# A fourth seven-product chunk pair in each feed-forward block, its raw-weight split put first, and the read-back cast queued behind a weight cast

## Chip, cores and metric

One core of one Trainium2 chip. The metric is the device time of one execution, in microseconds (us); lower is better. Three runs of the kernel before gave 2432.48, 2436.15 and 2436.17 us.

## What is computed

The forward pass of two layers of a transformer-like trunk on 256 tokens of width 2048, in float32. Each layer does `x += mixer(rmsnorm(x))`, `x += swiglu(rmsnorm(x))` and a gated embedding term; a last RMSNorm ends it. The change is in the feed-forward part alone:

```python
def _swiglu(h, norm_g, w_gate, w_up, w_down):
    xn = _rmsnorm(h, norm_g)
    return (jax.nn.silu(xn @ w_gate) * (xn @ w_up)) @ w_down
```

The hidden width is 5632, so `w_gate` and `w_up` are 2048 x 5632 and `w_down` is 5632 x 2048, in each of the two layers. The batch is one sequence, two tiles of 128 tokens.

## The kernel before

**Matmuls.** Float32 products are made of three matmuls in a reduced format. A weight tile is split into a high part (`whi`, a cast on ScalarE, ACT, L106) and a low part (`wlo`, the raw tile minus the high part, on VectorE, DVE, L107), and the activations are held split in the same way. The product is high x high, high x low and low x high: three matmuls of 128x128 by 128x512 into one PSUM bank. Splits are made for two chunks of 128 rows at a time (1024 columns). `whi` and `wlo` have four buffers each.

**Units.** `unit` (L209) loads four chunks (1 MB) by one DMA on SyncE's queue (SP, L218) into a raw tile, splits them in two halves, and runs 24 matmuls: four chunks, two token tiles, three matmuls. There are three raw tiles in turn; a transfer into one waits for the splits that read it last. After each half `tick` counts one, and may run one piece of deferred work from a queue (`later`), which names the least number of ticks to wait. Program order is a priority for the tile scheduler, which then fixes an order on each engine's queue by its own model of time; each engine works through its queue in order.

**Feed-forward.** `ffn` (L827) goes over 11 blocks of 512 hidden columns in groups of three (the last group has two). For each block it makes gate and up (`gate_up`), and from the second group on the down products of the group before are done in between: one or two "down blocks" of 12 chunks (72 matmuls, three units) after each block. So blocks 0 to 3 follow each other without one, block 3 is followed by one, and so on; four stand behind the last block.

**Block 0** is all units (`gate_up_8`). During its second half `sums_of_operand` (L835) makes four combinations of the first `2 * NS` chunks of the activations, and splits them into `ST`.

**Blocks 1 to 10** (`gate_up_7`, L880) take the first `2 * NS` chunks in pairs. A pair is two chunks times two weights (gate, up) times two token tiles: eight products, which are made from seven by a scheme of the kind of Strassen's. `pair` (L851) loads the raw weights of two chunks of gate and of up by two DMAs (L855) into one raw tile, makes four sums of them on DVE in `T` (L858 with 1024 columns, L859 and L860 with 512 each), and splits seven pieces of 512 columns, two at a time, for seven products into seven PSUM banks (L849). The banks are B1 to B7. B1, B2 and B4 use the activations as they are, and B3, B5, B6 and B7 their combinations `ST`. The other chunks are done by units, `classical`, in the banks of B2, B4, B3 and B22; a unit stands between any two pairs.

With `NS = 3` a block has three pairs (63 matmuls) and units over chunks 6 to 15 of each weight: four units of four chunks and two of two (120 matmuls), 183 in all. Two units stand between the pairs and the rest behind them. Behind the last pair the shared sums are formed from B1, B5, B6 and B7 in `E` (a copy on ACT at L893, DVE at L894 to L897). L902 adds banks 0 and 1 (gate), then, when the units of the up weight are done, banks 2 and 3. L906 is the silu and L931 the product with the gate. `T` and `E` share one buffer, `work`.

**Turning the hidden block.** `cross` (L138) transposes the block of hidden values in 32x32 tiles on DVE (L143), writes it to DRAM by four DMAs of GpSimd's queue (POOL, L147) and reads it back by two (L151) as `tx`. `split_hid` (L919) splits what came back into `hH` (a cast on ACT, L921) and `hL` (DVE, L922), the stationary operand of the down blocks. `cross` is deferred by two ticks behind the block, and `split_hid` until 16 ticks behind `cross`:

```python
            later(lambda: x.update(x=cross(sl, fp)), key=("xT", i, b))
            later(lambda: split_hid(hT[gi], x["x"], 4 * n), key=("hT", i, b), after=(("xT", i, b), 16))
```

A pair makes two ticks, a unit of four chunks two, a unit of two chunks one. A block makes 16, a down block six.

Of the kernel before, what the change touches and what calls it, by code (L numbers as in the profile page):

```python
# [27 lines left out]
def trunk_kernel(ctx: ExitStack, tc: tile.TileContext, x, p, even_norm, even_w_in, even_w_gk,  # L28
# [74 lines left out]
    got_gains = turn_gains(0, graw)  # L103

    def split_sb(raw, hi, lo):
        nc.scalar.copy(hi, raw)  # L106
        nc.vector.tensor_tensor(lo, raw, hi.bitcast(F32), OP.subtract)  # L107


# [711 lines left out]

    NS = 3
    B2, B4, B3, B22, B1, B5, B6, B7 = range(8)

    def ffn(i, xs, nkey, nx_fn, fp):  # L827
# [19 lines left out]
        def product(p, stat, hi, lo, first, last):  # L847
            for m, (a, b) in enumerate(((stat[0], hi), (stat[0], lo), (stat[1], hi))):
                nc.tensor.matmul(bank[:, p], a, b, start=first and m == 0, stop=last and m == 2)  # L849

        def pair(j, b):  # L851

            raw = raw_tile().rearrange("p (r c) n -> p r c n", r=2)
            for c, w in enumerate((ffn_w_gate[i], ffn_w_up[i])):
                nc.sync.dma_start(raw[:, :, c], w[2 * j * P:(2 * j + 2) * P, b * NB:(b + 1) * NB]  # L855
                                  .rearrange("(k q) n -> q k n", q=P))

            nc.vector.tensor_tensor(T[:, 0:2], raw[:, 0], raw[:, :, 1], OP.add)  # L858
            nc.vector.tensor_tensor(T[:, 2], T[:, 1], raw[:, 0, 0], OP.add)  # L859
            nc.vector.tensor_tensor(T[:, 3], T[:, 2], raw[:, 1, 0], OP.add)  # L860

            def tok(c, t):
                return [x[:, 2 * j + c, t * P:(t + 1) * P] for x in xs]

            def comb(n):
                return [ST[:, hl, n, j] for hl in range(2)]

            pieces = [(raw[:, 0, 0:1], [(B1, tok(0, 0))]), (T[:, 0:2], [(B5, comb(0)), (B7, comb(2))]),
                      (T[:, 2:4], [(B6, comb(1)), (B4, tok(1, 1))]),
                      (raw[:, 1], [(B2, tok(1, 0)), (B3, comb(3))])]  # L870
            for n, (src, ps) in enumerate(pieces):
                hi = wp.tile([P, 2, NB], F32R, name="whi")
                lo = wp.tile([P, 2, NB], F32R, name="wlo")
                split_sb(src, hi[:, :len(ps)], lo[:, :len(ps)])
                for c, (p, stat) in enumerate(ps):
                    product(p, stat, hi[:, c], lo[:, c], j == 0, j == NS - 1 and p >= B1)
                if n % 2:
                    tick()

        def gate_up_7(b):  # L880
            need(("sT", i))
            rest = [(n, k) for n in range(2) for k in range(2 * NS, KC, KU)]

            def classical(n, k):
                nk = min(KU, KC - k)
                unit([bank[:, 2 * n], bank[:, 2 * n + 1]], xs, k, [((ffn_w_gate[i], ffn_w_up[i])[n], b * NB, NB)],
                     n == 1 and k == 2 * NS, k + nk == KC, nk=nk, begun=1)

            for j in range(NS):
                pair(j, b)  # L890
                if j < NS - 1:
                    classical(*rest.pop(0))
            nc.scalar.copy(E[:, 0], bank[:, B1])  # L893
# [24 lines left out]

        def split_hid(dst, x, k0):  # L919
            d = [dst[n][:, k0:k0 + 4, :].rearrange("p m (q r) -> p m q r", q=8) for n in range(2)]  # L920
            nc.scalar.copy(d[0], x)  # L921
            nc.vector.tensor_tensor(d[1], x, d[0].bitcast(F32), OP.subtract)  # L922

        def gate_up(gi, n):
# [7 lines left out]
                                               op1=OP.mult)  # L932
            x = {}
            later(lambda: x.update(x=cross(sl, fp)), key=("xT", i, b))
            later(lambda: split_hid(hT[gi], x["x"], 4 * n), key=("hT", i, b), after=(("xT", i, b), 16))

        def down(gi, cb, nx):
            for b in groups[gi]:
# [176 lines left out]
```

## Time and profile before

| | |
|---|---|
| median of three runs | 2436.15 us |
| lowest, highest | 2432.48, 2436.17 us |
| the profiled execution | 2435.57 us |
| its span in the trace | 2433.9 us |
| mean granted TensorE clock | 0.995 |
| TensorE (PE) busy | 2393.8 us |
| VectorE (DVE) busy | 1716.8 us |
| ScalarE (ACT) busy | 1258.4 us |
| GpSimd (POOL) busy | 105.6 us |

The profile is of one execution. PE is matmuls, and PEld the weight loads that overlap them. Matmuls overlap each other, so that a busy time is counted once and a matmul's own duration (0.39 us) is longer than the step from one to the next. The granted clock is what the throttle let TensorE have, as a share of full speed. "Idle before" an instruction is the time in which its engine did nothing ahead of it, with what ended that; a DMA lands later than the row of its issue. In the views below L849 is the matmuls of the pairs, and L235 to L237 those of the units.

### The profile page before, as it was taken

To read this page: it belongs to the slowest core of one execution; us is meant where nothing else is said; L and a number is where in the kernel's file an instruction comes from. 1 tells how busy PE (TensorE), PEld (TensorE's weight loads), DVE (VectorE), ACT (ScalarE), POOL (GpSimd) and SP (SyncE) were. 2 spreads that over 40 slices of the span, in tenths; PEclk is the share of its full clock that TensorE was granted. 3 is DMA by queue.
4 is the path that set the end of the run, shared out by engine and by line. 5 is a ranking of instruction groups with operands and counts; after the bars stand their busy time and mean duration, and the time that the engine had idled before them with its cause. 6 is when DMAs were issued, how large, how long until landed. Compare 5 with 4: busy or idle time off the path is not lost.

```text
span 2433.9 us, 28109 instructions
## 1 busy us (share of the span) xinstructions
PE 2393.8 (98%) x10786; PEld 1965.1 (81%) x10786; DVE 1716.8 (71%) x2009; ACT 1258.4 (52%) x1560; POOL 105.6 (4%) x177
## 2 busy tenths in 40 slices
PE   8999999999999999999999999999999999999998
PEld 7887788778887788888888888887788887888887
DVE  5765556888877877756666666568888788777565
ACT  6644445555545545446546565545554454454463
POOL 0000100100000000000000000000000000000000
PEclk9999999999999999999999999999999999999999
DMA  6454465566666666555554555555666666666563
GB/s 211 146 170 147 147 208 189 194 213 207 213 228 207 208 225 225 196 194 182 176 188 158 169 174 172 193 189 186 203 215 218 217 207 209 223 225 206 183 232 123
DMA packets 240681, 473.13 MB, mean 194 GB/s; under 512 B 12849, under 2 KB 19729, under 8 KB 240418
## 3 DMA queue, kind: packets, MB, share of 16 engines
q1 hardware_dynamic: 232514, 447.07, 55.5%
q0 software_dynamic: 7744, 23.08, 3.0%
q8 instruction: 84, 1.38, 0.2%
q10 hardware_dynamic: 288, 1.18, 0.1%
q14 instruction: 51, 0.42, 0.1%
HBM read 457.66 MB, written 13.63 MB: 194 GB/s over the span
## 4 chain that ended last, share of the span: by engine, by line
PE 71%; DVE 11%; DMA 10%; ACT 3%; issue 3%; SPq 0%; POOL 0%; DVEq 0%; POOLq 0%; ACTq 0%
PE bank L236 20%; PE bank L235 20%; PE bank L237 20%; PE bank L849 6%; DMA raw<-in_ffn_w_up_dram 6%; DVE wlo L107 6%; DMA raw<-in_odd_w_in_dram 2%; ACT whi L106 1%; DVE kT L135 1%; PE bank L165 1%; DVE work L858 1%; DMA raw<-in_ffn_w_down_dram 1%; DMA tx<-ty 1%; DVE sl L931 1%; DVE work L902 1%
## 5 line engine op out<-in xcount | busy, mean ns | idle before, releaser
L107 DVE TENSOR_TENSOR wlo<-raw,whi 128x1024 fp32r<-128x1024 f32 (+2 forms) x848 | 981.7, 1172 | 460.1 <-ACT whi L106 456.4
L106 ACT CAST whi<-raw 128x1024 fp32r<-128x1024 f32 (+2 forms) x848 | 842.3, 1011 | 830.6 <-PE bank L237 542.3
L235 PE MATMUL bank<-whi,aH 128*128 128x512 f32 (+2 forms) x2176 | 849.7, 391 | 0.7 <-ACT whi L106 0.7
L236 PE MATMUL bank<-wlo,aH 128*128 128x512 f32 (+2 forms) x2176 | 843.6, 388 | 5.0 <-DVE wlo L107 5.0
L237 PE MATMUL bank<-whi,aL 128*128 128x512 f32 (+2 forms) x2176 | 842.9, 388 | 0.0
L236 PEld LDWEIGHTS bank<-wlo,aH 128*128 128x128 f32 x2176 | 410.0, 188 | 89.5 <-DVE wlo L107 8.9
L235 PEld LDWEIGHTS bank<-whi,aH 128*128 128x128 f32 x2176 | 409.8, 188 | 84.9 <-issue 2.8
L237 PEld LDWEIGHTS bank<-whi,aL 128*128 128x128 f32 x2176 | 409.4, 188 | 84.9 <-issue 1.0
L235 PE MATMUL bank<-whi,hH 128*128 128x512 f32 x704 | 277.2, 394 | 0.0
L236 PE MATMUL bank<-wlo,hH 128*128 128x512 f32 x704 | 277.0, 393 | 0.0
L237 PE MATMUL bank<-whi,hL 128*128 128x512 f32 x704 | 273.6, 389 | 0.0
L106 ACT CAST whi<-work 128x1024 fp32r<-128x1024 f32 x120 | 126.3, 1053 | 199.5 <-PE bank L237 122.8
L107 DVE TENSOR_TENSOR wlo<-work,whi 128x1024 fp32r<-128x1024 f32 x120 | 146.7, 1222 | 58.0 <-ACT whi L106 57.6
L849 PE MATMUL bank<-whi,sT 128*128 128x512 f32 x480 | 170.2, 394 | 5.5 <-ACT whi L106 5.5
L235 PEld LDWEIGHTS bank<-whi,hH 128*128 128x128 f32 x704 | 132.2, 188 | 30.0
L237 PEld LDWEIGHTS bank<-whi,hL 128*128 128x128 f32 x704 | 132.1, 188 | 29.7
L236 PEld LDWEIGHTS bank<-wlo,hH 128*128 128x128 f32 x704 | 132.4, 188 | 26.1
L849 PEld LDWEIGHTS bank<-whi,sT 128*128 128x128 f32 x480 | 91.2, 190 | 25.3 <-ACT whi L106 6.3
L858 DVE TENSOR_TENSOR work<-raw 128x1024 f32<-128x1024 f32 x60 | 73.4, 1224 | 52.0 <-DMA raw<-in_ffn_w_up_dram 51.6
L147 POOL DMA_DIRECT2D ty<-tq x88 | 48.6, 559 | 1123.3 <-DVE tq L143 973.0
L849 PE MATMUL bank<-wlo,sT 128*128 128x512 f32 x240 | 94.8, 395 | 1.9 <-DVE wlo L107 1.9
L849 PE MATMUL bank<-wlo,aH 128*128 128x512 f32 x180 | 73.3, 407 | 10.8 <-DVE wlo L107 10.4
(253 smaller groups left out, 1623.9 us busy)
## 6 DMA issues: line engine op xcount, KB each, us to landing
raw<-in_ffn_w_down_dram SPq DMA_DIRECT2D x88, 1024.0 KB, 5.4
raw<-in_ffn_w_gate_dram SPq DMA_DIRECT2D x48, 1024.0 KB, 5.2
raw<-in_ffn_w_up_dram SPq DMA_DIRECT2D x48, 1024.0 KB, 5.2
raw<-in_odd_w_in_dram SPq DMA_DIRECT2D x48, 1024.0 KB, 5.1
raw<-in_ffn_w_gate_dram SPq DMA_DIRECT2D x80, 512.0 KB, 4.1
raw<-in_ffn_w_up_dram SPq DMA_DIRECT2D x80, 512.0 KB, 5.3
raw<-in_even_w_in_dram SPq DMA_DIRECT2D x36, 1024.0 KB, 5.1
raw<-in_ple_w_gate_dram SPq DMA_DIRECT2D x28, 1024.0 KB, 5.1
```

The source lines that it names most:

```text
L106: nc.scalar.copy(hi, raw)
L107: nc.vector.tensor_tensor(lo, raw, hi.bitcast(F32), OP.subtract)
L135: nc.vector.transpose(dst[32 * a:32 * a + 32, :, :, 32 * q:32 * q + 32], src.rearrange("p t (m a c) -> p t m a c", a=4, c=32)[32 * q:32 * ...
L147: nc.gpsimd.dma_start(y[:, :, q].rearrange("a c t n -> c a (t n)"), tq[32 * q:32 * q + 32].rearrange("c a t m r -> c a (t m r)"))
L165: nc.tensor.transpose(ps[:, c, tt, :], h[:, tt, k * P:(k + 1) * P], ident)
L235: nc.tensor.matmul(ps[tt][:, :n], sh, hi[:, c, :n], start=st, stop=False)
L236: nc.tensor.matmul(ps[tt][:, :n], sh, lo[:, c, :n], start=False, stop=False)
L237: nc.tensor.matmul(ps[tt][:, :n], sl, hi[:, c, :n], start=False, stop=en)
L849: nc.tensor.matmul(bank[:, p], a, b, start=first and m == 0, stop=last and m == 2)
L858: nc.vector.tensor_tensor(T[:, 0:2], raw[:, 0], raw[:, :, 1], OP.add)
L902: nc.vector.tensor_tensor(e, bank[:, 2 * n:2 * n + 2], e, OP.add)
L931: nc.vector.scalar_tensor_tensor(sl[:, tt], pu[tt], rs[:, tt:tt + 1], sl[:, tt], op0=OP.mult, op1=OP.mult)
```

## The change

`NS` goes from 3 to 4, so that a block takes chunks 0 to 7 in four pairs (84 matmuls) and chunks 8 to 15 in four units of four chunks (96 matmuls): 180 in all. Three of the units stand between the pairs, the third of them already a unit of the up weight, and one stands behind the last pair. Where a bank's accumulation ends is now worked out from what is left, since the gate's units end before the last pair. The combinations of the activations are four thirds as wide.

Within a pair the seven pieces are taken in another order. The first is now both gate weights as loaded (B1 and B2); then the first two sums are made and split (B5, B7), then the last two (B6, B4), and the last piece is one weight as loaded (B3). Before, all sums stood ahead of the first split, which was one weight (B1), and the last piece had two (B2, B3).

The cast of the hidden block read back, L921, gets an edge in ACT's queue behind the last weight cast that was traced before it (`state["cast"]`, kept by `split_sb`), and is traced 10 ticks behind `cross` in place of 16.

```diff
     def split_sb(raw, hi, lo):
-        nc.scalar.copy(hi, raw)
+        state["cast"] = nc.scalar.copy(hi, raw).ins
         nc.vector.tensor_tensor(lo, raw, hi.bitcast(F32), OP.subtract)
...
-    NS = 3
+    NS = 4
...
-        def pair(j, b):
+        def pair(j, b, rest):
...
-            nc.vector.tensor_tensor(T[:, 0:2], raw[:, 0], raw[:, :, 1], OP.add)
-            nc.vector.tensor_tensor(T[:, 2], T[:, 1], raw[:, 0, 0], OP.add)
-            nc.vector.tensor_tensor(T[:, 3], T[:, 2], raw[:, 1, 0], OP.add)
+            def sums_13():
+                nc.vector.tensor_tensor(T[:, 0:2], raw[:, 0], raw[:, :, 1], OP.add)
+
+            def sums_24():
+                nc.vector.tensor_tensor(T[:, 2], T[:, 1], raw[:, 0, 0], OP.add)
+                nc.vector.tensor_tensor(T[:, 3], T[:, 2], raw[:, 1, 0], OP.add)
...
-            pieces = [(raw[:, 0, 0:1], [(B1, tok(0, 0))]), (T[:, 0:2], [(B5, comb(0)), (B7, comb(2))]),
-                      (T[:, 2:4], [(B6, comb(1)), (B4, tok(1, 1))]),
-                      (raw[:, 1], [(B2, tok(1, 0)), (B3, comb(3))])]
-            for n, (src, ps) in enumerate(pieces):
+            pieces = [(None, raw[:, :, 0], [(B1, tok(0, 0)), (B2, tok(1, 0))]),
+                      (sums_13, T[:, 0:2], [(B5, comb(0)), (B7, comb(2))]),
+                      (sums_24, T[:, 2:4], [(B6, comb(1)), (B4, tok(1, 1))]),
+                      (None, raw[:, 1, 1:2], [(B3, comb(3))])]
+            for n, (made, src, ps) in enumerate(pieces):
+                if made:
+                    made()
...
                 for c, (p, stat) in enumerate(ps):
-                    product(p, stat, hi[:, c], lo[:, c], j == 0, j == NS - 1 and p >= B1)
+                    product(p, stat, hi[:, c], lo[:, c], j == 0,
+                            j == NS - 1 and (p >= B1 or not any(n == p // 2 for n, _ in rest)))
...
         def split_hid(dst, x, k0):
             d = [dst[n][:, k0:k0 + 4, :].rearrange("p m (q r) -> p m q r", q=8) for n in range(2)]
-            nc.scalar.copy(d[0], x)
+            with tc.issue_after(state["cast"]):
+                nc.scalar.copy(d[0], x)
             nc.vector.tensor_tensor(d[1], x, d[0].bitcast(F32), OP.subtract)
...
-            later(lambda: split_hid(hT[gi], x["x"], 4 * n), key=("hT", i, b), after=(("xT", i, b), 16))
+            later(lambda: split_hid(hT[gi], x["x"], 4 * n), key=("hT", i, b), after=(("xT", i, b), 10))
```

## Rows read from the trace of the kernel before

**Rows 1.** The page of the profile: its head, and busy time by engine.

```profile
span 2433.9 us, 28109 instructions
...
PE 2393.8 (98%) x10786; PEld 1965.1 (81%) x10786; DVE 1716.8 (71%) x2009; ACT 1258.4 (52%) x1560; POOL 105.6 (4%) x177
```

**Rows 2.** Busy time by stretch (instructions), then granted clock, DMA share and GB/s.

```profile
core 0: us, PE busy (x) PEld busy (x) DVE busy (x) ACT busy (x) POOL busy (x), PEclk, DMA share, GB/s
433.30:584.30 151.00, 145.64 (x623) 118.03 (x622) 127.48 (x133) 77.64 (x84) 15.03 (x24) 0.98 0.65 216
584.30:987.40 403.10, 399.89 (x1748) 327.09 (x1747) 313.14 (x319) 199.96 (x211) 22.21 (x36) 1.00 0.65 211
1645.00:1799.50 154.50, 147.23 (x622) 119.01 (x621) 128.10 (x133) 77.65 (x84) 14.85 (x24) 0.97 0.64 211
1799.50:2203.10 403.60, 400.00 (x1748) 327.04 (x1747) 314.04 (x320) 199.89 (x211) 22.23 (x36) 1.00 0.64 211
718.10:776.10 58.00, 58.00 (x256) 47.88 (x256) 43.99 (x46) 29.07 (x31) 3.64 (x6) 1.00 0.65 209
477.20:525.50 48.30, 45.15 (x184) 36.12 (x183) 39.44 (x42) 24.01 (x26) 3.70 (x6) 0.93 0.61 196
1691.50:1740.80 49.30, 45.15 (x185) 35.97 (x184) 39.69 (x42) 24.00 (x26) 3.70 (x6) 0.93 0.59 192
525.30:555.80 30.50, 30.35 (x133) 24.45 (x132) 29.18 (x32) 17.01 (x19) 3.70 (x6) 1.00 0.61 205
389.00:433.30 44.30, 44.30 (x201) 36.65 (x200) 30.40 (x35) 21.97 (x27) 3.01 (x1) 1.00 0.56 179
```

**Rows 3.** Timeline of PE in block 2 of either layer (start, us, instruction).

```profile
499.88 0.39 PE L849 MATMUL bank<-whi,sT 128*128 128x512 f32 x1
502.61 0.79 PE L849 MATMUL bank<-whi,sT 128*128 128x512 f32 x1 [2.34 <-ACT whi L106]
...
1717.88 0.79 PE L849 MATMUL bank<-whi,sT 128*128 128x512 f32 x1 [3.13 <-ACT whi L106]
```

**Rows 4.** Timeline of ACT at the same two places.

```profile
500.57 1.04 ACT L921 CAST hH<-tx 128x1024 fp32r<-128x1024 f32 x1 [5.35 <-DMA tx<-ty]
...
1715.83 1.04 ACT L921 CAST hH<-tx 128x1024 fp32r<-128x1024 f32 x1 [6.13 <-DMA tx<-ty]
```

**Rows 5.** Who waited for whom: us in total, times, longest.

```profile
DVE work L858 <- DMA raw<-in_ffn_w_up_dram: 51.6, 37, 4.5
...
ACT hH L921 <- DMA tx<-ty: 14.4, 4, 6.1
...
PE bank L849 <- DVE wlo L107: 12.3, 17, 3.0
...
PE bank L849 <- ACT whi L106: 5.5, 2, 3.1
```

**Rows 6.** Timeline of DVE at the end of block 3.

```profile
547.77 1.22 DVE L922 TENSOR_TENSOR hL<-tx,hH 128x1024 fp32r<-128x1024 f32 x1
548.91 1.22 DVE L107 TENSOR_TENSOR wlo<-raw,whi 128x1024 fp32r<-128x1024 f32 x1
550.04 0.68 DVE L894 TENSOR_TENSOR work<-bank,work 128x512 f32<-128x512 f32 x1
550.64 1.22 DVE L107 TENSOR_TENSOR wlo<-raw,whi 128x1024 fp32r<-128x1024 f32 x1
551.77 0.68 DVE L895 TENSOR_TENSOR work<-bank,work 128x512 f32<-128x512 f32 x1
```

**Rows 7.** Instructions by line and shape (busy us, mean ns).

```profile
L106 ACT CAST whi<-raw 128x1024 fp32r<-128x1024 f32 x772 | 796.5, 1049 | 775.6 <-PE bank L237 512.8 <-DMA raw<-in_odd_w_in_dram 84.6 <-DMA raw<-in_ffn_w_up_dram 53.7
...
L106 ACT CAST whi<-raw 128x512 fp32r<-128x512 f32 x68 | 42.1, 621 | 49.9 <-PE bank L237 27.3 <-DVE wlo L107 10.1 <-PE bank L849 9.9
...
L931 DVE SCALAR_TENSOR_TENSOR sl<-work,rstd,sl 128x512 f32<-128x512 f32 x40 | 28.2, 746 | 0.0
...
L143 DVE STREAM_TRANSPOSE tq<-sl 128x1024 f32<-128x1024 f32 x22 | 27.3, 1242 | 0.3
```

More of the change, by code (lines that the diff above doesn't have):

```diff
@@ L881, in gate_up_7 @@
             need(("sT", i))
+            left = [NS]
             rest = [(n, k) for n in range(2) for k in range(2 * NS, KC, KU)]
@@ L886, in classical @@
                 unit([bank[:, 2 * n], bank[:, 2 * n + 1]], xs, k, [((ffn_w_gate[i], ffn_w_up[i])[n], b * NB, NB)],
-                     n == 1 and k == 2 * NS, k + nk == KC, nk=nk, begun=1)
+                     n == 1 and k == 2 * NS, k + nk == KC and (n == 1 or left[0] == 0), nk=nk, begun=1)
             for j in range(NS):
-                pair(j, b)
+                left[0] -= 1
+                pair(j, b, rest)
                 if j < NS - 1:
```

## The prediction

> **What bounds the kernel now.** The page comes first: TensorE is busy for 2393.8 of 2433.9 us, VectorE (DVE) for 1716.8, ScalarE (ACT) for 1258.4 [rows 1]. An average says little here, so the next view is busy time by stretch, cut at the blocks of the feed-forward layers [rows 2]. The stretch 718.1 to 776.1 us runs without a loss of TensorE: one block of 183 matmuls and one down block of 72, 255 in 58.00 us, so 0.2275 us a matmul. With this price each stretch splits into work and loss. The two feed-forwards have the same two kinds.
>
> Stretch A (433.3 to 584.3, and 1645.0 to 1799.5): blocks 1, 2 and 3 run back to back and one down block follows, 3 x 183 + 72 = 621 matmuls = 141.3 us. It takes 151.0 and 154.5 us: 9.7 and 13.2 us are lost. DVE is busy for 127.48 and 128.10 us of it.
>
> Stretch B (584.3 to 987.4, and 1799.5 to 2203.1): six blocks, each followed by one or two down blocks, nine in all, 1746 matmuls = 397.2 us. It takes 403.1 and 403.6: 12.3 us lost over 36 pairs, 0.34 us a pair. DVE has some 90 us of slack in each.
>
> Where does A lose? In block 2 of each layer: 48.30 and 49.30 us for 183 matmuls (41.6 us), a loss of 14.4 in the two [rows 2]. The TensorE timeline shows one place: no matmul for 2.34 us at 499.9 and for 3.13 us at 1714.4, and behind it matmuls of 0.79 in place of 0.39 us [rows 3]; the granted clock of these two stretches is 0.93, a part at the lower level of 1.2 GHz. TensorE waits for a weight cast on ACT, and that one is stuck behind the cast of the hidden block read back from DRAM, L921, which waits 5.35 and 6.13 us for its DMA [rows 4]. ACT works in order, so a cast put too early holds up all behind it. Of 22 such casts 4 wait, 14.4 us [rows 5].
>
> The remaining losses are small ones in the pairs: TensorE waits 17 times, 12.3 us, for the low half of a pair's weights, and DVE waits 37 times, 51.6 us, at L858 for the up half of the raw weights [rows 5].
>
> **The products.** A fourth pair replaces 24 matmuls by 21 in each of 20 blocks: 60 x 0.2275 = 13.65 us off TensorE. The first, fully coded block and the down blocks stay.
>
> **DVE.** A pair costs one sum and three splits of 1024 columns and two sums and one split of 512; it displaces two splits of 1024. Back to back these start 1.14 and 0.60 us apart (a single one shows 1.22 and 0.68, the end of it overlapping the next) [rows 6]. So +2 x 1.14 + 3 x 0.60 = +4.08 us a block, 82 us in all. ACT has one cast of 1024 and one of 512 more a block, 1.05 + 0.62 = 1.7 us [rows 7]; it is busy for half of each stretch and no bound. DVE decides where it has no cover. In A it rises by 3 x 4.08 = 12.2 to 139.7 and 140.3 us, while TensorE's work falls to 612 x 0.2275 = 139.2. The two are level, and a queue in order is never wholly full: the fullest stretch of this trace, 525.3 to 555.8, has DVE at 29.18 of 30.50 us, 0.957, with TensorE still busy for 30.35 [rows 2]. I take that share: 139.7 / 0.957 = 146.0. The bounds are 140 (DVE full) and 155 (0.90 of the time). To this I add 1.5 us for raw weights that come late at a pair, of the size of the L858 waits, and set A at 147.5 in each layer: -3.5 and -7.0, together -10.5. That holds the whole change in A, the read-back included.
>
> In B DVE rises by 24.5 to about 338 of some 400 us; the down blocks give the slack back. There, and in block 10 behind it, 14 blocks save 3 x 0.2275 = 0.68 each: -9.55. Against it stand 14 more pairs at up to 0.34 us, +4.8 if a pair stalls as before. The bounds are +15 (every seam below costs 1 us) and -12.3 (all pair stalls go); I take half of the old price, +2.4, because of the next part.
>
> **Split first.** In the old order all three sums stand ahead of the first split in the program, and L858 has to wait for the up half. Now the first piece is both gate weights as they are: 6 matmuls, 1.37 us, can start without any sum, and the sums are made where they are needed. The last piece is a single product. Work is unchanged but for the order; price between -12 (the stalls of rows 5 go) and 0, and half of the pairs' price is its share above.
>
> **The end of a block.** The four combining sums, L893 to L897, and the first L902 now have 24 matmuls (5.46 us) behind the last pair in place of 72 (16.4 us). On DVE they take 4 x 0.60 + 1.14 = 3.5 us, and in the trace they are interleaved with splits [rows 6]. With a down block behind, the two splits of the last unit and these sums fit: 5.8 us against 5.46 plus the 1.4 us between the B6 product and the pair's end. With another pair behind (blocks 1 to 2, 2 to 3) they do not, and that is part of what 0.957 in A covers.
>
> **The read-back.** The cast L921 moves behind the last weight cast traced ten ticks after its transfer was issued; a unit of four or a pair makes two ticks, so 5 units, 27 us of TensorE. Casts run up to four buffers ahead, at most 48 matmuls or 10.9 us, so it comes some 16 us or more behind the transpose. In the trace it was tried at 500.57 - 5.35 = 495.2 and had to wait until 500.5. The wait goes; left over would be 0 to 2 us of ACT, which the four buffers cover. Behind L921 stand the weight casts, as before; L922 on DVE and the down block wait for it. The tightest case is block 10, whose values are wanted 24 matmuls behind the two down blocks that the ten ticks fill: 5.5 us against 1.05 + 1.22 us of cast and subtraction. Without this cover it costs about 2.3 us a layer. POOL's four writes and two reads per block stay where they are.
>
> **Raw weights.** SP's queue issues 12 transfers a block before and after, the same 8 MB; nine raw tiles become eight. No charge. The operand sums at the start grow by a third, some 1.6 us on DVE a layer, in a stretch where DVE has 30.40 of 44.30 us [rows 2] and TensorE loses nothing: no charge.
>
> **The sum.** -10.5 (A) - 9.55 + 2.4 (B and block 10) = -17.7 us. The profiled execution took 2435.57 us (span 2433.9), 0.58 under the median of 2436.15; so 2417.9 for its like, and 2418 as the median.
>
> **Rivals.** (1) *The seam is the bound, and it gets slower.* At the end of every block DVE has the sums, the last adds, L931, the transpose [rows 7] and the next splits within 24 matmuls. For it: 0.60 x 4 + 1.14 x 2 + 1.4 + 1.2 + two splits 2.3 + a pair 6.4 = 16 us of DVE stand against 5.46 + 4.78 = 10.2 us of TensorE. Against it: splits done ahead, and a down block behind 16 of 20 blocks. If 2 us are lost in each of 20 seams, 40 us stand against 13.65 + 13 gained: +13, 2449. It decides from 1.35 us a seam. In the trace the gaps of 2.34 and 3.13 us were followed by matmuls of 0.79 us [rows 3] and a granted clock of 0.93 over the block [rows 2]. The Trainium skill ("TensorE: Matmul & The Clock Gate", Part 1) says that the low clock is the default and activity releases it; by that rule a seam with such a gap would be paid twice, once idle and once slow, and the trace agrees: 0.93. Chance 0.17.
>
> (2) *DVE eats the products in A and half of B.* A gives -6 in all (13 us of read-back stalls go, 7 come back as waits for DVE) and B -3: 2427. For it: 139.7 against 139.2. The Trainium skill ("Perfetto Trace Analysis", Identifying the Most-Contended Engine) would have the fullest engine relieved first; in A that would be DVE, to which this change adds. Chance 0.15.
>
> (3) *The queueing does nothing*, since the cast stays where a late DMA holds it: 13 us less gain, 2431. Against it: the edge is to a cast 27 us further on. Chance 0.06.
>
> (4) *Most pair stalls go too*, as no split waits behind a sum any more: A at 146.0 (-5.0 and -8.5), B and block 10 at -9.55 and two thirds of B's 12.3 us less: -31, 2405. For it: the 51.6 us of L858's waits; against it: more of DVE in each pair. Chance 0.12.
>
> **How the numbers follow.** My forecast has 0.50. Predicted 2418. The range takes in rival 4 and bounds of A below, rivals 2 and 3 and the lesser half of rival 1 above: 2403 to 2441; its own range, with A from 143 to 153 us in each layer and B by 3 us either way, is 2406 to 2432. About 0.2%, 4.9 us, is what a measurement of this kernel tells from none. Faster: 0.50 + 0.12 + most of rivals 2 and 3 = 0.74; within: 0.10; slower: rival 1 but for its mildest part, 0.16.
>
> **What would show it.** Right: 60 matmuls fewer; no ACT wait of L921 for tx; granted clock 1.00 in block 2; A near 147 and B near 400 us with DVE over 0.93 of A. Wrong: gaps of TensorE between the last pair of a block and the next, waiting for wlo; L894 to L902 ahead of splits that TensorE waits for; L858 waits no fewer and longer.

## The result, and the profile after

The changed kernel takes **2455.5 us** (median of 4 runs, 2450.18 to 2456.48) where the kernel before took 2436.16 beside it: a ratio of 1.0073, 95% interval [1.0055, 1.0091]. It is slower, by 0.7% and clear of the noise; 2418 was forecast, with 0.16 for slower. The profiled execution (2450.18 us) is the shortest of the four, so the stretches below show some 5 us less loss than the median run has.

The page of the changed kernel, its head and busy time by engine, against [rows 1]:

```profile
span 2448.5 us, 28193 instructions
...
PE 2387.4 (98%) x10726; PEld 1954.8 (80%) x10726; DVE 1800.9 (74%) x2109; ACT 1300.1 (53%) x1600; POOL 101.7 (4%) x177
```

The work changed as forecast: TensorE has 60 matmuls fewer, VectorE is busy for 84 us more (82 were reckoned). The time went elsewhere. Busy time by stretch, cut as in [rows 2] (first stretch A, then B, in either layer; then block 2, and block 3 with its down block):

```profile
433.10:588.00 154.90, 144.87 (x613) 114.52 (x612) 136.98 (x145) 82.92 (x90) 15.03 (x24) 0.99 0.63 208
588.00:995.70 407.70, 397.49 (x1729) 324.76 (x1728) 340.81 (x352) 212.55 (x223) 22.21 (x36) 1.00 0.64 210
1652.80:1807.40 154.60, 145.38 (x614) 115.48 (x613) 137.18 (x146) 83.08 (x90) 14.85 (x24) 0.98 0.62 209
1807.40:2217.70 410.30, 399.82 (x1729) 327.32 (x1728) 341.00 (x352) 212.60 (x223) 22.23 (x36) 0.99 0.63 209
...
476.40:522.00 45.60, 42.79 (x182) 33.32 (x181) 42.91 (x46) 25.17 (x28) 3.70 (x6) 1.00 0.62 209
522.00:588.00 66.00, 60.34 (x253) 47.78 (x252) 56.53 (x60) 34.25 (x37) 7.40 (x12) 0.97 0.63 206
```

A went from 151.0 and 154.5 to 154.9 and 154.6, where 147.5 stood in the forecast; B from 403.1 and 403.6 to 407.7 and 410.3, where some 400 stood. What lies outside A and B is 1321.0 us, and was 1321.7. So 3.9 + 0.1 + 4.6 + 6.7 - 0.7 = 14.6 us, the difference of the two spans, arose in the feed-forwards, though TensorE has 13.65 us less to do there. Some 28 us are new loss. By the 0.2275 us a matmul of the prediction, some 8 of them arose in A, although the read-back's stalls went from there, and 19.5 in B (14.6 and 17.2 us lost, 12.3 before). Block 2, which lost 6.7 us to the read-back, is better (45.60 us for 180 matmuls, 41.0 us of work). Who waited for whom, against [rows 5] (the first line is of the kernel before, whose L860 is the same instruction as L862 here):

```profile
ACT whi L106 <- DVE work L860: 24.1, 8, 4.1
...
ACT whi L106 <- DVE work L862: 82.2, 30, 4.9
...
DVE work L858 <- DMA raw<-in_ffn_w_up_dram: 66.9, 47, 3.4
...
PE bank L849 <- DVE h L268: 17.5, 8, 2.6
...
PE bank L849 <- ACT whi L106: 10.6, 6, 3.6
```

VectorE's waits for the up half grew (51.6 before); ScalarE waits more than three times as long as before for the last sum of a pair, L862; and TensorE has a wait that it hardly had before (0.5 us), for L268, the addition of a down block to h. ScalarE's wait by itself is no loss: two faster kernels further down have 135.2 and 109.7 us of it.

**First place, the seam without a down block.** TensorE's timeline from block 2 to block 3 (the first line is the last matmul before the gap):

```profile
525.40 0.40 PE L849 MATMUL bank<-whi,sT 128*128 128x512 f32 x1
529.41 0.80 PE L849 MATMUL bank<-whi,sT 128*128 128x512 f32 x1 [3.61 <-ACT whi L106]
530.00 0.63 PE L849 MATMUL bank<-whi,aH 128*128 128x512 f32 x1
530.67 0.80 PE L849 MATMUL bank<-wlo,sT 128*128 128x512 f32 x1
```

VectorE over the same seam:

```profile
518.13 0.69 DVE L903 TENSOR_TENSOR work<-bank,work 128x512 f32<-128x512 f32 x1
518.73 1.22 DVE L107 TENSOR_TENSOR wlo<-raw,whi 128x1024 fp32r<-128x1024 f32 x1
519.87 0.69 DVE L904 TENSOR_TENSOR work<-bank,work 128x512 f32<-128x512 f32 x1
520.47 0.68 DVE L905 TENSOR_TENSOR work<-bank,work 128x512 f32<-128x512 f32 x1
521.07 2.35 DVE L910 TENSOR_TENSOR work<-bank,work 128x1024 f32<-128x1024 f32 x2
523.33 1.22 DVE L107 TENSOR_TENSOR wlo<-work,whi 128x1024 fp32r<-128x1024 f32 x1
524.46 1.41 DVE L940 SCALAR_TENSOR_TENSOR sl<-work,rstd,sl 128x512 f32<-128x512 f32 x2
525.79 0.68 DVE L861 TENSOR_TENSOR work<-work,raw 128x512 f32<-128x512 f32 x1
526.39 1.24 DVE L143 STREAM_TRANSPOSE tq<-sl 128x1024 f32<-128x1024 f32 x1
527.55 0.65 DVE L862 TENSOR_TENSOR work<-work,raw 128x512 f32<-128x512 f32 x1
```

And ScalarE's cast that TensorE waits for:

```profile
528.31 1.04 ACT L106 CAST whi<-work 128x1024 fp32r<-128x1024 f32 x1 [4.60 <-DVE work L862]
```

The granted clock behind the gap:

```profile
529.00:533.00 4.00, 3.55 (x8) 2.41 (x9) 3.95 (x5) 2.99 (x5) 1.18 (x4) 0.57 0.71 146
```

From 518 to 528 us VectorE is never idle. What it does is the end of block 2 (L903 to L905, both L910, L940, L143) mixed with the splits and sums of the first pair of block 3. All the sums that end a block stand within and just behind the one unit of 24 matmuls that is left behind its last pair. L862, which the third cast of the next block's first pair needs, comes last. Behind the gap the matmuls start 0.59 and 0.67 us apart in place of 0.2275, at a granted clock of 0.57. The other layer has the same gap of 3.61 us between its blocks 2 and 3; between blocks 1 and 2 the gaps are 1.46 and 1.47 us.

**Second place, the first pair behind a lone down block** (blocks 4, 5, 7 and 8 of each layer, eight places, the 17.5 us of the waits above). TensorE:

```profile
588.47 0.39 PE L849 MATMUL bank<-whi,aL 128*128 128x512 f32 x1
591.45 0.50 PE L849 MATMUL bank<-whi,aH 128*128 128x512 f32 x1 [2.60 <-DVE h L268]
```

VectorE at the same place:

```profile
588.44 1.23 DVE L858 TENSOR_TENSOR work<-raw 128x1024 f32<-128x1024 f32 x1 [3.37 <-DMA raw<-in_ffn_w_up_dram]
589.58 1.22 DVE L107 TENSOR_TENSOR wlo<-work,whi 128x1024 fp32r<-128x1024 f32 x1
590.71 1.28 DVE L268 TENSOR_TENSOR h<-bank,h 128x512 f32<-128x512 f32 x2
```

The pair's second product now goes into bank 0, which the down block holds until L268 has read it. The down block's last matmul starts at 587.78, so L268 is ready soon after, but it stands in VectorE's queue behind an L858 (that of the second pair) whose transfer is late, and behind a split that waits there too. The Trainium skill ("PSUM — Partial Sum Buffer", Engine vs sequencer instructions) says that VectorE's queue is strictly first in, first out; these rows agree: 2.60 us of TensorE for an addition of 0.68 us that had nothing left to wait for.

### The profile page after: what moved, and what is told of

Read it like the earlier page. It is cut to its first block, busy times and chain, and to the rows that moved or that the text cites. A ratio compares the mean times of both kernels' runs of the same rounds, so it can differ in the third digit from the quotient of the medians.

```text
span 2448.5 us, 28193 instructions
## 1 busy us (share of the span) xinstructions
PE 2387.4 (98%) x10726; PEld 1954.8 (80%) x10726; DVE 1800.9 (74%) x2109; ACT 1300.1 (53%) x1600; POOL 101.7 (4%) x177
## 4 chain that ended last, share of the span: by engine, by line
PE 68%; DVE 15%; DMA 10%; issue 4%; ACT 3%; SPq 1%; DVEq 0%; ACTq 0%; POOLq 0%; POOL 0%
PE bank L236 19%; PE bank L237 18%; PE bank L235 18%; PE bank L849 8%; DMA raw<-in_ffn_w_up_dram 8%; DVE wlo L107 7%; DVE work L858 2%; ACT whi L106 1%; DMA raw<-in_odd_w_in_dram 1%; DVE kT L135 1%; PE bank L165 1%; DVE sl L940 1%; DVE work L861 1%; DVE work L910 1%; DVE tq L143 0%
## 5 line engine op out<-in xcount | busy, mean ns | idle before, releaser
L236 PE MATMUL bank<-wlo,aH 128*128 128x512 f32 (+2 forms) x2016 | 782.8, 388 | 12.4 <-DVE wlo L107 12.0
L235 PE MATMUL bank<-whi,aH 128*128 128x512 f32 (+2 forms) x2016 | 788.1, 391 | 0.6 <-ACT whi L106 0.6
L237 PE MATMUL bank<-whi,aL 128*128 128x512 f32 (+2 forms) x2016 | 780.3, 387 | 0.0
L236 PEld LDWEIGHTS bank<-wlo,aH 128*128 128x128 f32 x2016 | 379.3, 188 | 96.7 <-DVE wlo L107 22.7
L106 ACT CAST whi<-work 128x1024 fp32r<-128x1024 f32 x160 | 167.9, 1049 | 206.4 <-PE bank L237 102.0
L236 PE MATMUL bank<-wlo,hH 128*128 128x512 f32 x704 | 277.0, 393 | 0.0
L107 DVE TENSOR_TENSOR wlo<-work,whi 128x1024 fp32r<-128x1024 f32 x160 | 195.2, 1222 | 62.9 <-ACT whi L106 62.6
L849 PE MATMUL bank<-whi,sT 128*128 128x512 f32 x640 | 230.3, 400 | 10.2 <-ACT whi L106 10.2
L849 PEld LDWEIGHTS bank<-whi,sT 128*128 128x128 f32 x640 | 123.5, 193 | 37.9 <-ACT whi L106 12.3
L236 PEld LDWEIGHTS bank<-wlo,hH 128*128 128x128 f32 x704 | 132.4, 188 | 26.1
L858 DVE TENSOR_TENSOR work<-raw 128x1024 f32<-128x1024 f32 x80 | 97.9, 1223 | 67.2 <-DMA raw<-in_ffn_w_up_dram 66.9
L849 PE MATMUL bank<-wlo,sT 128*128 128x512 f32 x320 | 129.1, 404 | 4.3 <-DVE wlo L107 4.1
L849 PE MATMUL bank<-whi,aH 128*128 128x512 f32 x240 | 95.4, 397 | 17.9 <-DVE h L268 17.5
```

The costliest lines, as they stand in the source:

```text
L106: state["cast"] = nc.scalar.copy(hi, raw).ins
L235: nc.tensor.matmul(ps[tt][:, :n], sh, hi[:, c, :n], start=st, stop=False)
L236: nc.tensor.matmul(ps[tt][:, :n], sh, lo[:, c, :n], start=False, stop=False)
L237: nc.tensor.matmul(ps[tt][:, :n], sl, hi[:, c, :n], start=False, stop=en)
```

## The experiments

**The bank alone.** The lone down block goes into the banks that a pair writes fifth and sixth (B6 and B4, its third piece); the rest is the changed kernel.

```diff
-        def down(gi, cb, nx):
+        def down(gi, cb, nx, ps=None):
...
-            ps = block(hT[gi], [(ffn_w_down[i], cb * NB, NB)], nk=nk, kw=groups[gi][0] * 4)
+            ps = block(hT[gi], [(ffn_w_down[i], cb * NB, NB)], nk=nk, kw=groups[gi][0] * 4, ps=ps)
...
+                        down(gi - 1, cb, None, [bank[:, B6], bank[:, B4]] if len(cbs) == 1 else None)
```

> The changed kernel, but the down block that stands alone between two blocks accumulates in the banks of B6 and B4 in place of banks 0 and 1 (bank 0 is B2's, which the next pair's first piece writes 0.7 us after its start). Theory 1 (the bank: the pair's second product waits for the down block's sum L268, which DVE does late, 8 times, 20.8 us of steps less 8 x 0.23 = 18.8 us in the changed kernel's trace): 13 to 17 us less than the changed kernel, median 2438 to 2443, ratio to the kernel before 1.001 to 1.003, no wait for L268 over 1 us. Theory 2 (the seam: DVE is behind in every block, and a wait taken away comes back as a wait for wlo): not under 2450.

Measured: 2444.0 us, ratio 1.0024 [1.0013, 1.0036]; B 404.5 and 406.1. Three waits:

```profile
DVE work L858 <- DMA raw<-in_ffn_w_up_dram: 76.7, 49, 3.4
...
PE bank L849 <- DVE h L268: 2.7, 6, 0.7
...
PE bank L236 <- DVE wlo L107: 22.0, 29, 1.2
```

The wait for L268 falls from 17.5 to 2.7 us, and 12 of the 18 us of slowdown go; the ratio is in theory 1's range, the median 1 us above it. The bank costs something, but the late transfers stay, part of the wait comes back at the units (TensorE's waits for wlo at L236 were 12.0 us in the changed kernel), and the kernel is still slower than before with 13.65 us less work.

**Four pairs in the old order** (all sums first, bank 0 last), with the read-back's change:

```diff
+            sums_13()
+            sums_24()
-            pieces = [(None, raw[:, :, 0], [(B1, tok(0, 0)), (B2, tok(1, 0))]),
+            pieces = [(None, raw[:, 0, 0:1], [(B1, tok(0, 0))]),
...
+                      (None, raw[:, 1], [(B2, tok(1, 0)), (B3, comb(3))])]
```

> The changed kernel (four pairs, read-back cast queued) with the old order in a pair: all sums first, then B1 alone, and B2 in the last piece. Theory 1 (the bank): B2 comes 3.4 us later in the pair and the waits for L268 go: 2435 to 2443. Theory 2 (the seam: a fourth pair's DVE work is the cost, in whatever order): 2450 to 2458.

Measured: 2463.55 us, 1.0110 [1.0090, 1.0131]; A 162.9 and 161.5. This is above the ranges of both theories. The new order is not what costs: without it the kernel is some 9 us (0.0037) slower still.

**The read-back alone** (three pairs, the old order of the last diff, the cast tied behind the last weight cast, ten ticks):

```diff
-    NS = 4
+    NS = 3
...
             with tc.issue_after(state["cast"]):
                 nc.scalar.copy(d[0], x)
```

> The kernel before with the read-back cast alone changed (edge behind a weight cast, 10 ticks): three pairs, old order. If the read-back wait is a loss by itself, as predicted: 10 to 14 us faster than before, 2422 to 2427, with no ACT wait of the cast for tx. Rival (the time is lost to the next late thing): 2433 to 2438.

Measured: 2444.69 us, 1.0028 [1.0016, 1.0040]. ScalarE no longer waits for tx, and yet the kernel is slower than before, above both ranges. VectorE in block 2 of this run:

```profile
492.15 1.23 DVE L858 TENSOR_TENSOR work<-raw 128x1024 f32<-128x1024 f32 x1 [2.96 <-DMA raw<-in_ffn_w_up_dram]
```

and TensorE:

```profile
494.57 0.50 PE L849 MATMUL bank<-wlo,sT 128*128 128x512 f32 x1 [2.48 <-DVE wlo L107]
```

The time came back one engine on: in the old order the next pair's sums stand ahead of the split that TensorE needs, and they wait for the up half. Such a gap stands in blocks 2 and 3 of both layers (2.48, 2.49, 2.54 and 2.40 us), where the kernel before, apart from a gap in block 1 that both kernels have, lost 2.34 and 3.13 us in block 2 alone.

**The order alone** (three pairs; the read-back as before, 16 ticks):

```diff
-    NS = 4
+    NS = 3
...
-            with tc.issue_after(state["cast"]):
-                nc.scalar.copy(d[0], x)
+            nc.scalar.copy(d[0], x)
```

> The kernel before with the order in the pair alone changed (both gate weights' split first, sums behind it): three pairs, read-back cast as before. Theory 1 (the bank): the waits for L268 are there with three pairs too, 8 of about 2 us: 2447 to 2456. Theory 2 (the fourth pair's DVE work): 2428 to 2438.

Measured: 2427.31 us, **0.9958 [0.9943, 0.9972]**, faster; A 149.0 and 148.5. The order gains 10 us, a little more than theory 2 allowed, with the L268 wait still in it (7.9 us in 8 places).

**Sums tied behind the split.** If sums that wait for the up half hold up VectorE's queue, they can be tied behind the split that the program puts ahead of them:

```diff
-        nc.vector.tensor_tensor(lo, raw, hi.bitcast(F32), OP.subtract)
+        state["lo"] = nc.vector.tensor_tensor(lo, raw, hi.bitcast(F32), OP.subtract).ins
...
-                    made()
+                    with tc.issue_after(state["lo"]):
+                        made()
```

In the changed kernel:

> The changed kernel with each pair's sums queued on DVE behind the split ahead of them in the program, so that L858 cannot stand ahead of splits and sums of the work before it while it waits for its raw weights (in the changed kernel L858 waits 66.9 us, 47 times). Theory 1 (DVE's order: what stands behind a waiting L858 comes late, L268 and the wlo of the pair before): the waits of TensorE for L268 fall under half of their 18.8 us and those for wlo too, 2425 to 2440. Theory 2 (DVE's throughput in the seams is the bound whatever the order): 2450 to 2460.

with the two banks as well:

> The same with the lone down block in the banks of B6 and B4. Theory 1: 2420 to 2435, and under the sums-pinned kernel by 3 to 8 us, as L268 is off TensorE's way. Theory 2: not under 2440, as with the banks alone (2444).

with three pairs, the banks, and the read-back as before:

> Three pairs, split first, sums pinned, lone down block in the banks of B6 and B4, read-back cast as before the change. Theory 1: stretch A keeps only the read-back stalls (some 13 us), so 2415 to 2422, under split first alone (2427). Theory 2: no gain over split first alone, 2425 to 2430.

and the same with the read-back's change:

> The same three pairs with the read-back cast queued as in the change. Theory 1: with L858 out of the way the read-back edge now gives what it should, 8 to 13 us less than the three-pair kernel without it, 2405 to 2413, and less than the four-pair kernel with pinned sums and banks by what DVE costs in A. Theory 2 (the queueing of the cast costs by itself, as its first run, 6 us slower than before, may be read): 2422 to 2435.

Measured: 2501.59 (1.0280 [1.0264, 1.0295]), 2498.42 (1.0264 [1.0247, 1.0281]), 2454.1 (1.0082 [1.0067, 1.0097]) and 2461.16 (1.0113 [1.0098, 1.0128]). All four are far slower than any figure expected ("not under 2440" of the second holds, but by 58 us). Against the same kernels without the tie they lose 0.0207, 0.0240, 0.0150 and 0.0195; the last two of these comparisons are with runs that follow below. Two waits of the first:

```profile
ACT whi L106 <- DVE work L858: 218.3, 80, 3.6
...
ACT whi L106 <- DVE work L862: 177.3, 78, 3.7
```

No L858 waits for a transfer any more, but each pair now hands over from VectorE to ScalarE and back, one after the other: the sums' lead was worth more than their waits cost.

**The fourth pair, and the read-back in the new order.** Two runs complete the table of the three parts, a third adds the banks to the order alone. The first is the changed kernel with the read-back undone:

```diff
-            with tc.issue_after(state["cast"]):
-                nc.scalar.copy(d[0], x)
+            nc.scalar.copy(d[0], x)
...
-            later(lambda: split_hid(hT[gi], x["x"], 4 * n), key=("hT", i, b), after=(("xT", i, b), 10))
+            later(lambda: split_hid(hT[gi], x["x"], 4 * n), key=("hT", i, b), after=(("xT", i, b), 16))
```

> Four pairs and the new order as in the changed kernel, the read-back's cast and due time as before. The changed kernel stands at a ratio of 1.0073, three pairs in the new order without the read-back's change at 0.9958: 28 us lie between, and two parts of the change. Theory 1: the parts add up, and the read-back's change costs the 6 us that it cost alone; so this comes at about 2454 - 6 = 2448, a ratio of about 1.005, and the fourth pair is what costs some 22 us. Theory 2: the fourth pair is worth its 12.6 us of products as forecast and the read-back's change eats it: a ratio of 0.990 to 0.996, 2412 to 2427. On theory 1 stretch A is 152 to 155 us with hardly fewer VectorE waits for the up transfer than the changed kernel's 46 us; on theory 2 it is 145 to 149.

The second is the changed kernel with `NS = 3`:

> Three pairs in the new order with the read-back's change. Theory 1 (the parts add up, the read-back's change costs about 6): a ratio of 0.998 to 1.000, about 2433, with waits of the sums for the next pair's up transfer in blocks 1 to 3 where the cast used to wait. Theory 2 (the read-back's change is what eats the fourth pair's gain): a ratio of 1.002 to 1.008. A third possibility: in the new order the split that stands ahead of the sums covers the new wait, and the read-back's change gains what it was forecast to: 0.990 to 0.993, stretch A at 144 to 146 us.

The third is the order alone with the banks of the first experiment:

> Three pairs in the new order, no change to the read-back, and the down block that stands alone between two gate-and-up blocks put into the two banks that a pair writes third and fourth. The trace of the same kernel with the old banks has 9.2 us of TensorE waits for the down block's addition to h over 8 places, all in stretch B. Theory 1 (the bank is why): these fall to under 2 us and the time by 5 to 9 us, to a ratio of 0.992 to 0.9935, about 2419. Theory 2 (VectorE is behind there and the bank only names it): the waits pass to the weight pieces and the ratio stays at 0.9945 to 0.9965.

Measured: 2467.2 us, 1.0128 [1.0114, 1.0142]; 2417.27 us, **0.9920 [0.9906, 0.9933]**; 2421.39 us, 0.9932 [0.9920, 0.9945]. Together:

| pairs | order | read-back | ratio |
|---|---|---|---|
| 3 | old | before | 1 |
| 3 | old | changed | 1.0028 |
| 4 | old | changed | 1.0110 |
| 3 | new | before | 0.9958 |
| 3 | new | changed | **0.9920** |
| 4 | new | before | 1.0128 |
| 4 | new | changed | 1.0073 (the change) |

The fourth pair costs 0.0153 with the read-back's change and 0.0170 without it, 37 and 41 us; the read-back's change costs 0.0028 in the old order and gains 0.0038 and 0.0055 in the new one. In the old order, with the read-back's change, the fourth pair costs 0.0082, 20 us (four pairs in the old order with the read-back as before were not run); so part of its cost is where it meets the new order, and the banks below bear that out. Both theories of the first expectation are off: in the new order the fourth pair costs nearly twice what theory 1 said, and the read-back gains, which is the third possibility of the second. In the third run the banks gain 0.0026 on top of the order, as its theory 1 says. In the second run no cast waits for tx. In the first it does, more than in the kernel before (14.4):

```profile
ACT hH L929 <- DMA tx<-ty: 39.5, 10, 7.0
```

A and B (first layer) of the run with three pairs, new order and read-back:

```profile
433.10:577.00 143.90, 142.92 (x622) 115.94 (x621) 127.80 (x132) 78.87 (x84) 15.00 (x24) 1.00 0.68 227
577.00:979.00 402.00, 399.53 (x1748) 327.14 (x1747) 315.97 (x321) 203.05 (x211) 22.17 (x36) 1.00 0.65 212
```

A has 621 matmuls, 141.3 us, and takes 143.9: nearly no loss is left.

**All three gains with three pairs** (the second run above with the banks):

> Three pairs, the new order, the read-back's change, and the lone down block in the two other banks: the three edits of which each has gained by itself or on top of the new order (ratios 0.9958 for the order, 0.992 with the read-back, 0.9932 with the banks). If the gains add up: 0.9958 - 0.0038 - 0.0026 = 0.989 to 0.990, about 2412. If the two last ones recover the same lost time: 0.991 to 0.993.

Measured: 2415.92 us, 0.9918 [0.9904, 0.9932]. The banks add nothing that can be told on top of the read-back. Four pairs against three, both with the banks, is 1.0024 against 0.9918: the fourth pair costs 0.0106 there, in place of 0.0153.

**What the fourth pair's cost hangs on.** Three kernels. In the changed kernel one unit of four chunks is moved from between the last two pairs to behind the last pair; no engine's work changes:

```diff
-                if j < NS - 1:
+                if j < NS - 2:
                     classical(*rest.pop(0))
```

> The changed kernel with one unit of four chunks moved from between the last two pairs to behind the last pair: 48 matmuls in place of 24 cover the combining sums, and the work of every engine is the same. Theory S (the fourth pair costs what it does because the block's end has too little cover): the TensorE gaps at the seams between blocks go, and the time falls from 2455 by 15 to 35 us, to a ratio of 0.993 to 1.001. Theory W (the fourth pair's VectorE work as such, 4.08 us a block, is what is too much): the gaps move to the two pairs that now stand side by side, and the ratio stays at 1.005 to 1.012.

Or the unit is taken from between the first two pairs:

```diff
-                if j < NS - 1:
+                if 0 < j < NS - 1:
                     classical(*rest.pop(0))
```

> As the one before, but the unit is taken from between the first two pairs, so that these stand side by side at the start of a block. Theory S: again 15 to 35 us less than the changed kernel, within 8 us of the one before. Theory W: 1.005 to 1.015. If only the pairs side by side matter, the two differ: here they come right behind the former block's sums, so this one is the slower by over 8 us.

Or, in the kernel of three pairs with order and read-back, VectorE gets the work of a fourth pair and nothing else:

```diff
-                nc.vector.tensor_tensor(T[:, 0:2], raw[:, 0], raw[:, :, 1], OP.add)
+                for _ in range(2):
+                    nc.vector.tensor_tensor(T[:, 0:2], raw[:, 0], raw[:, :, 1], OP.add)
...
-                nc.vector.tensor_tensor(T[:, 2], T[:, 1], raw[:, 0, 0], OP.add)
+                for _ in range(1 + (j == 0)):
+                    nc.vector.tensor_tensor(T[:, 2], T[:, 1], raw[:, 0, 0], OP.add)
```

> Three pairs, the new order and the read-back's change (ratio 0.992), with VectorE work added that nothing needs: the sum of each pair is made twice and one short sum a block, 3 x 1.14 + 0.60 = 4.02 us a block, what a fourth pair adds to VectorE. TensorE, ScalarE, the transfers and the order are unchanged. Theory W: 15 to 40 us slower, a ratio of 0.998 to 1.008. Theory S: the work lies in the slack behind 72 matmuls of classical units, and the ratio stays at 0.992 to 0.996.

Measured: 2424.0 us, **0.9946 [0.9933, 0.9958]**; 2419.38 us, **0.9930 [0.9917, 0.9942]**; 2439.0 us, 1.0012 [1.0003, 1.0020]. One unit moved is worth 31 and 35 us of the changed kernel's time. Where a block's units stand is the larger cause (theory S), with both runs in its ranges; the work as such (theory W) is a cause too, 0.0092 or 22 us for 80 us of it. The two overlap and can't be added: together they are more than the fourth pair cost. Nor is either pure. The unit behind the last pair may also give the next transfers more time (L858's waits fall from 66.9 to 40.7 us with the cover from the back), and the wait for L268 falls with it, to 5.6 us and to nothing; what each is worth was not tried apart. The added sums stand ahead of casts that wait for the sums, so ScalarE waits longer as well (92.8 us for the first sums, 37.5 without the added work). With the cover from the back the gap of 3.61 us is gone from both layers. TensorE has no wait for a cast at a pair any more; its waits for VectorE's splits, the longest 1.4 us, stand at the units:

```profile
PE bank L236 <- DVE wlo L107: 20.3, 21, 1.4
```

Where each acts, the stretches tell. A and B of the first layer with the cover from the back:

```profile
435.60:584.70 149.10, 142.57 (x614) 113.85 (x613) 138.65 (x147) 83.07 (x90) 15.03 (x24) 1.00 0.67 218
584.70:986.10 401.40, 396.01 (x1730) 323.62 (x1729) 341.68 (x351) 211.72 (x223) 22.21 (x36) 1.00 0.65 212
```

with the cover from the front:

```profile
432.70:587.10 154.40, 147.80 (x613) 117.73 (x612) 141.60 (x148) 82.55 (x90) 15.03 (x24) 0.96 0.63 211
587.10:982.30 395.20, 394.62 (x1730) 324.12 (x1729) 339.60 (x350) 211.49 (x223) 22.22 (x36) 1.00 0.65 216
```

and with the added work:

```profile
434.20:586.50 152.30, 145.71 (x623) 115.09 (x622) 140.25 (x144) 76.77 (x84) 15.03 (x24) 1.00 0.64 214
586.50:989.70 403.20, 400.12 (x1747) 326.86 (x1746) 339.33 (x345) 201.94 (x211) 22.21 (x36) 1.00 0.65 211
```

In A, where three blocks run back to back, the added work costs 8.4 us (143.90 to 152.30) and four pairs cost 5.2 (4.4 in the other layer) in the better of the two orders: there VectorE is short. In B the same work costs 1.2 us (4.5 in the other layer), and four pairs with their cover from the front take 395.20 us, for 1728 matmuls that are 393.1 us of work: there it was mostly the order that was wrong. In that run the second pair's transfer is also issued one step earlier, right behind the first pair's, and L858's waits fall to 12.2 us and that for L268 to nothing; with the cover from the back they are 40.7 and 5.6. How much of B's last 6 us is the cover and how much the earlier transfer was not tried apart. In A the same order takes 154.40 us against 149.10, and not because TensorE is idle for longer: 6.6 us (154.40 - 147.80) against 6.5 (149.10 - 142.57). The same matmuls are busy for 5.2 us longer, at a granted clock of 0.96 against 1.00. The clock falls behind two stalls at the start of blocks 2 and 3. TensorE there, in block 2:

```profile
482.62 0.50 PE L849 MATMUL bank<-wlo,aH 128*128 128x512 f32 x1 [1.53 <-DVE wlo L107]
...
484.90 1.22 PE L849 MATMUL bank<-whi,sT 128*128 128x512 f32 x2 [1.09 <-ACT whi L106]
```

Two pairs side by side meet the sums of the block before, with no down block between them.

**Pairs where there is cover for them.** Three pairs in blocks 1 to 3, four in the later ones with the cover from the front:

```diff
-            left = [NS]
-            rest = [(n, k) for n in range(2) for k in range(2 * NS, KC, KU)]
+            ns = 3 if b < 4 else NS
+            left = [ns]
+            rest = [(n, k) for n in range(2) for k in range(2 * ns, KC, KU)]
...
-                if j < NS - 1:
+                if ns - 4 < j < ns - 1:
```

> Three pairs in blocks 1 to 3, which run back to back, and four in the later blocks, there with the first two pairs side by side and 48 matmuls behind the last; the new order and the read-back's change throughout. Theory S, put together from stretches: A as with three pairs and the read-back's change (143.9 and 144.5 us), B as in the run with the cover taken from the front (395.1 and 395.2): 2419.4 - 10.5 - 9.6 = 2399, a ratio of 0.984 to 0.987. If the gain of B hung on how A ends (splits done ahead, raw weights early) it comes out at 0.988 to 0.992.

Measured: 2401.77 us, **0.9856 [0.9840, 0.9872]**, 34 us less than the kernel before and 54 less than the change as it was made. Its stretches:

```profile
434.00:577.60 143.60, 142.61 (x623) 116.02 (x623) 128.45 (x133) 78.89 (x84) 15.00 (x24) 1.00 0.67 227
577.60:972.80 395.20, 394.67 (x1729) 324.02 (x1728) 340.04 (x350) 211.36 (x223) 22.17 (x36) 1.00 0.65 216
1630.70:1774.20 143.50, 142.52 (x622) 116.06 (x621) 128.45 (x133) 78.87 (x84) 14.81 (x24) 1.00 0.67 227
1774.20:2169.70 395.50, 394.80 (x1730) 324.06 (x1729) 339.98 (x350) 211.38 (x223) 22.19 (x36) 1.00 0.65 216
```

A and B came out as put together from two other runs, within 1.0 and 0.4 us; 2399 was expected. VectorE is busier by 26 to 27 us in either B than in the kernel before, and TensorE, with 393.1 us of work, loses some 2 us.

## Why the prediction was wrong

**The end of a block** is the step that failed; in the sum it stands behind the +2.4 for B, which lost 19.5 us more than before, and is part of the 147.5 for A, which took 154.9 and 154.6. It saw that the sums and the first L910 (the first L902 before) would have 24 matmuls behind the last pair in place of 72, and let the seams with a down block behind pass as covered: 5.8 us of VectorE against 5.46 + 1.4 of TensorE. That counts only what TensorE needs to end the block. It leaves out that VectorE's queue has by then to hold the next block's first splits and sums too, and that what it falls behind within a block is made up only behind the last pair. One unit moved there, work unchanged, is worth 0.0127 and 0.0143, 31 and 35 us; how these divide between the backlog, the wait for L268 and the late transfers stays open. The seams were said to decide from 1.35 us each (the terms given there make it 1.33); the fourth pair's 37 us, with the 13.65 us of products that it saved on top, would be 2.5 us for each of 20 seams. Rival 1 had this mechanism, this sign, and 2449 us; I gave it 0.17 because splits are done ahead and 16 of 20 blocks have a down block behind them. Those down blocks did not protect the seam as the program stood: at eight of the sixteen 17.5 us went to L268.

**DVE.** The work was right (+82 reckoned, +84 measured); the share that it can reach was not. I took 0.957 from a stretch of 30.50 us. In A of the first layer the changed kernel reached 136.98 / 154.90 = 0.884; with the cover moved it is 138.65 / 149.10 = 0.930, and 140.25 / 152.30 = 0.921 with three pairs and added work. At 0.93 A would be 139.7 / 0.93 = 150.2, not 146.0; and no order that was run brought A to 147.5 with four pairs.

**The products.** Right as a count. Worth having only where VectorE has slack: in B, and there mainly with the cover from the front (402.0 with three pairs to 395.2; 401.4 with the cover from the back).

**Split first.** Right in sign and size: -12 to 0 was the bound, -10 us was measured alone. But "Work is unchanged but for the order" missed one thing: the order also moved the product into bank 0 from the last piece to the first, and so took the cover from L268. That is 0.0049 (12 us) in the changed kernel, 0.0026 with the order alone, and nothing that can be told with three pairs and the read-back.

**The read-back.** The wait went, as said: ScalarE has no wait for tx in the changed kernel. "Left over 0 to 2 us" held only beside the new order: alone it cost 0.0028, as L858's waits took the wait's place; with the order and three pairs it brought A to 143.9 and 144.5. Two parts of the change that I had priced one by one depend on each other: the order gains alone, the read-back's change only beside it. The Trainium skill ("Perfetto Trace Analysis", Optimization Strategy) says that where the fullest engine changes over time, interleaving the regimes can help. Here a pair is VectorE's regime and a unit of four chunks TensorE's, and the runs don't bear that out at this size: the changed kernel puts a unit between any two pairs, and both kernels that put two pairs side by side, to have two units behind the last one, are faster by 0.0127 and 0.0143.

**Raw weights.** "No charge" was wrong in its effect: L858's waits went from 51.6 to 66.9 us. That they fall to 12.2 with the same bytes and the same VectorE work in another order shows that the order made the transfers late, and not the bytes alone.

## What to carry to other kernels

An engine that falls behind in one part of a loop body needs a part where it catches up, and here the work that was taken off the bound engine had been just that part: before trading TensorE work for VectorE work, count what stands behind the last dense piece, for the end of this block and the start of the next together. Where a resource such as a bank or a queue place is taken earlier than before, look up who holds it then and what that one stands behind. And price parts of a change that meet on the same queue together: here the read-back's change cost alone and gained beside the new order, and the fourth pair cost 0.0082 in one order and 0.0153 in the other.

## What the runs showed of the hardware

The length of a stall alone does not decide whether TensorE's clock drops. With the cover from the front, stalls of 1.53 and 1.09 us, with 1.2 us of matmuls between them, were followed by these stretches (granted clock in the third column from the end):

```profile
484.00:487.00 3.00, 1.87 (x4) 1.06 (x5) 2.92 (x4) 2.60 (x4) 0.00 (x0) 0.57 0.72 273
487.00:491.00 4.00, 4.00 (x11) 3.13 (x10) 3.33 (x4) 1.81 (x2) 1.50 (x2) 0.50 0.41 95
```

In the changed kernel the single stall of 2.60 us behind the matmul of 588.47 was not:

```profile
591.00:595.00 4.00, 3.55 (x16) 2.94 (x17) 3.96 (x7) 2.11 (x2) 0.00 (x0) 1.00 0.25 52
```

Yet four of its other seven waits for L268, of 2.13, 2.29, 2.46 and 2.56 us, were followed by a granted clock of 0.50, and three, of 1.71 to 1.94 us, were not. At 0.50, the lower level of 1.2 GHz, the matmuls start 0.42 to 0.43 us apart (at 487.37, 487.80 and 488.22 with the cover from the front), where they start 0.2275 apart at the higher one.

That is how A with the cover from the front came to a granted clock of 0.96, and there a stall is paid twice, once idle and once slow.
